# Moving two activation tiles by 896 bytes in on-chip memory, in a two-layer float32 decoder trunk

## Chip, cores and metric

The kernel runs on one core of one Trainium2 chip. The metric is the device time of one execution in microseconds. The inputs are float32, and most products run as three float32r matmuls on split operands (below).

## What is computed

512 tokens of 1,024 channels pass two layers. Layer 0 mixes tokens by a diagonal state-space model with a gated output, layer 1 by differential attention over shared keys and values. Behind each mixer stand a gated feed-forward part and a gated per-layer input. Cut to what matters here:

```python
x = x + s5_mixer(rms_norm(x, ssm_norm))        # w_in, state space, w_glu (1024 x 2048)
k, v = shared_kv(x, kv_norm, kv_w, k_norm)     # layer 1: kv_w (1024 x 2048)
x = x + diff_attention(rms_norm(x, attn_norm), k, v, ...)   # w_q, w_o (1024 x 1024)
for each layer, behind its mixer:
    up = rms_norm(x, ffn_norm) @ w_up          # 1024 x 5632, then a causal convolution of width 3
    x = x + (gelu(g) * val) @ w_down           # 2816 x 1024
    x = x + sigmoid(rms_norm(x, ple_norm) @ w_gate) * (p @ w_proj)
```

## The kernel before

**Products in three parts.** Every large product splits both operands into a float32r part and the float32r rest, and `mm3` (L115 to L120) adds three matmuls into one PSUM bank: high by high (L118), high of the stationary operand by rest of the moving one (L119), and rest by high (L120). Each of them loads a stationary operand of 128x128 and streams a moving operand of 512 columns (256 in a few places).

**Weights.** `stage` (L86) loads a block of 128x1024 into one of five `wst` tiles; `split` (L96) makes the high part on ScalarE (L102 or L107, tile `hi_wst`) and the rest on VectorE (L103 or L108, tile `lo_wst`), six buffers each.

**Activations.** `split_hT` (L160 to L166) writes the transposed activations of all 512 tokens into two constant tiles, `hTh` (high, by ScalarE) and `hTl` (rest, by VectorE), each of 8 k-tiles by 512 tokens, 16 KB a partition. All products with the 1,024 channels read them:
- `up` (the projection up): the weight is stationary, 128 columns of it, and a k-tile of `hTh` or `hTl` moves, 512 tokens.
- `pg` (per-layer gate), `u`, `gv`, `gg` (state-space input, value and gate blocks), `k`, `q`, `v`, `wo` (attention): 128 tokens of `hTh` or `hTl` are stationary, and 512 columns of a weight move. A block of 512 output columns is 4 token tiles x 8 k-tiles x 3 = 96 matmuls.

Two products do without them. `dn` (the projection down) has as stationary operand 128 tokens of `ih` or `il`, tiles of the feed-forward pool, and moves 512 columns of a weight. `pr` (the per-layer input) takes both operands from weight buffers, six matmuls a tile.

**Where tiles lie.** A pool lays its tiles one after another in the order in which they are made, so an address is the sum of what was made before. Start addresses in bytes of a partition, in the built program:

| tile | start | remainder by 256 |
|---|---|---|
| `ident`, `flip`, `junk`, `mhalf` | 16,512 to 19,584 | 128 |
| `x` (16,384 bytes) | 19,648 | 192 |
| `hTh` (16,384) | 36,032 | 192 |
| `hTl` (16,384) | 52,416 | 192 |
| `cw`, `neglam`, `qgain`, `gains` (704 + 32 + 32 + 128) | 68,800 to 69,568 | |
| `wst`, five of 4,096 | from 69,696 | 64 |
| `hi_wst`, six of 4,096 | from 90,176 | 64 |
| `lo_wst`, six of 4,096 | from 114,752 | 64 |
| `ih`, `il`, 14 each of 2,048 | from 164,416 and 193,088 | 64 |

An operand within a tile begins a multiple of 512 bytes behind the tile's start (1,024 where half the tokens move), so the remainder of the tile is that of every operand in it.

**Order of the work.** State space (`ssm`), feed-forward (`ffn`), per-layer input (`ple`), attention, feed-forward, per-layer input. The constant tiles are made in `Trunk.__init__` (L56 to L77); everything else follows from there.

Of the kernel before, what the change touches and what calls it, by code (L numbers as in the profile page):

```python
# [10 lines left out]
F32 = mybir.dt.float32  # L11
F32R = mybir.dt.float32r
# [6 lines left out]
P = 128  # L19
D = 1024  # L20
T = 512
# [12 lines left out]
# k-tiles of the second half of the state-space inputs, by the batch they follow  # L34
# [4 lines left out]
def two_pi_parts():  # L39
    """2 pi as parts of few bits, so that small multiples of the first ones are exact."""  # L40
    a = math.floor(2 * math.pi * 2 ** 9) / 2 ** 9
    b = math.floor((2 * math.pi - a) * 2 ** 21) / 2 ** 21
    return a, b, 2 * math.pi - a - b
# [9 lines left out]
class Trunk:  # L53
    def __init__(self, ctx, tc, io):
        self.tc, self.nc, self.io = tc, tc.nc, io
        nc = self.nc  # L56
        pool = lambda name, **k: ctx.enter_context(tc.tile_pool(name=name, **k))
        self.cpool = pool("const", bufs=1)
        self.wpool = pool("weights", bufs=6)
        self.npool = pool("norm", bufs=2)  # L60
        self.psum = pool("psum", bufs=1, space=PSUM)
        self.ident = self.cpool.tile([P, P], F32, name="ident")
        make_identity(nc, self.ident)
        self.flip = self.cpool.tile([P, P], F32, name="flip")
        self.junk = self.cpool.tile([P, D], BF16, name="junk")
        self.mhalf = self.cpool.tile([P, 16], F32, name="mhalf")
        nc.vector.memset(self.mhalf, -0.5)
        nc.scalar.activation(self.junk[:, :16], self.mhalf, AF.Sin)  # loads the table of the sine
        self.xall = self.cpool.tile([P, NT, D], F32, name="x")
        self.x = [self.xall[:, t, :] for t in range(NT)]  # L70
        self.hTh = self.cpool.tile([P, KD, T], F32R, name="hTh")
        self.hTl = self.cpool.tile([P, KD, T], F32R, name="hTl")
        self.cw = self.cpool.tile([P, 2 * NF, 4], F32, name="cw")
        self.neglam = self.cpool.tile([P, 1], F32, name="neglam")
        self.qgain = self.cpool.tile([P, 1], F32, name="qgain")
        self.gains = self.cpool.tile([P, 4, KD], F32, name="gains")
        self.nw = self.nb = 0  # L77
        self.later, self.turns, self.last = [], [], None
# [7 lines left out]
    def stage(self, src):  # L86
        """Loads [128, 1024] of a weight."""
        st = self.wpool.tile([P, 1024], F32, tag="wst", name=f"wst{self.nw}", bufs=5)
        self.nw += 1
        self.nc.sync.dma_start(st, src)  # L90
        return st
# [4 lines left out]
    def split(self, st, g=None):  # L96
        """A weight in two float32r parts; g: [128, 2], gains of its halves."""
        nc = self.nc
        hi = self.wpool.tile([P, 1024], F32R, tag="whi", name=f"hi_{st.name}")
        lo = self.wpool.tile([P, 1024], F32R, tag="wlo", name=f"lo_{st.name}")  # L100
        if g is None:
            nc.scalar.copy(hi, st)  # L102
            nc.vector.tensor_tensor(lo, st, hi.bitcast(F32), ALU.subtract)  # L103
            return hi, lo
        for k in range(2):
            c = slice(512 * k, 512 * k + 512)
            nc.scalar.activation(hi[:, c], st[:, c], AF.Copy, scale=g[:, k:k + 1])  # L107
            nc.vector.scalar_tensor_tensor(lo[:, c], st[:, c], g[:, k:k + 1], hi[:, c].bitcast(F32),  # L108
                                           ALU.mult, ALU.subtract)
        return hi, lo  # L110
# [11 lines left out]
    def norm(self, nm):  # L122
        """A function of t: the transpose of rms_norm(x) times the gain, for its 128 tokens, into hT."""
# [14 lines left out]
    def flush_turns(self, n=NT):  # L138
        """Emits the transposes of the first n normalized tiles that wait."""
        todo, self.turns = self.turns[:n], self.turns[n:]  # L140
        for f in todo:
            f()
# [9 lines left out]
    def turn(self, x, t, c, nm, tag="tp"):  # L152
        """The half c of the channels of x (128 tokens), transposed, into hT."""
# [6 lines left out]
    def split_hT(self, ps, k, t):  # L160
        """Four transposed blocks into the k-tiles from k on, for the 128 tokens t."""
# [9 lines left out]
    def ffn(self, i, nxt, order=(0, 1), before=None, after=None):  # L171
        """order: of the halves of the tokens at the start. before, after: what else to do on the way."""
# [80 lines left out]
    def ple(self, i, me, nxt=None):  # L253
        """Without nxt the results go out, the last ones in two parts."""
# [38 lines left out]
    # Four steps are a chunk; two groups (32 channels, 128 states) are a pair, four pairs a batch.  # L293
    # State at chunk ends: X[k] = A^4 X[k-1] + V[k]; with X[k] = Z[k] e^(i k phi) and phi the phase
    # of A^4, Z obeys a real recurrence. Outputs: y[4k+i] = C A^(i+1) X[k-1] + sum_j K[i-j] u[4k+j].
# [20 lines left out]
    def ssm_params(self, sp):  # L316
# [50 lines left out]
        # powers of A, as the coefficients of the outputs  # L367
# [18 lines left out]
        # input coefficients f A^(3-j), f = (A - 1) / lambda  # L386
# [12 lines left out]
        # phase of A^4 in turns, as a short and a small part; its multiples by 16 a and by b  # L399
# [27 lines left out]
    def exp(self, x, tl, itile):  # L427
        """e^x to float32's accuracy: 2^n times a polynomial of the rest."""
# [16 lines left out]
    def ssm_tables(self, sp, b):  # L445
        """cos and sin of k phi for the four pairs of a batch, [128, 4, 128]."""
# [22 lines left out]
    def cprod(self, sp, coef, mat, b, nm, conj):  # L469
        """coef[., q, n] * mat[., q, c] (complex) for a batch, [128, 2, 4, n, 16], or its conjugate."""  # L470
# [18 lines left out]
    def pad(self, dst, src):  # L489
        """Block-diagonal form over the two groups of a pair: dst [128, 8, n, 2, 16]."""  # L490
        for g in range(2):
            self.nc.scalar.activation(dst[:, :, :, g, :], src, AF.Copy, scale=self.maskS[:, g:g + 1])
# [6 lines left out]
    def ssm_prep(self, sp, b, coefs):  # L499
        """The stationary and moving operands of a batch: inputs to states, states and inputs to outputs."""  # L500
# [17 lines left out]
    def ssm_toep(self, sp, b, wp, op):  # L518
        """K[0..3] of a pair in the first 32 rows, then the lower rows shifted copies of them."""
# [19 lines left out]
    def ssm_turn_u(self, sp, b, U):  # L539
        """The inputs of a chunk as columns."""  # L540
# [8 lines left out]
    def ssm_inputs(self, b, uc, ctrl):  # L549
        """What the inputs of a chunk add to the states at its end."""  # L550
# [7 lines left out]
    def ssm_states(self, sp, b, v, tab):  # L558
        """The states before each chunk, as two products of the real part and of minus the imaginary part."""
# [27 lines left out]
    def ssm_out(self, sp, b, op, toep, uc, xs):  # L587
        """gelu of the outputs, [chunk, step, channel]."""
# [13 lines left out]
    def ssm_turn(self, b, g):  # L602
        """The k-tile b of the next product."""
# [10 lines left out]
    def ssm(self, nxt):  # L614
        nc, tc, io = self.nc, self.tc, self.io
        with ExitStack() as ctx:
# [3 lines left out]
            # tokens 4 k + j at [k, j]  # L620
# [30 lines left out]
            # software pipeline over the batches  # L651
# [63 lines left out]
    def tables(self):  # L715
        """rel: DRAM scratch [heads, 640]: column m is the bias at distance 511 - m, -1e30 below zero. neglam: [128, 1], minus lambda. qgain: [128, 1] over (c, d), the gain of the scaled query."""
# [20 lines left out]
    def strip(self, dst):  # L737
        """dst[p, h, r] = bias of head h at distance 511 - p - r; p is the place of a query from the end of 128."""
# [10 lines left out]
    def project(self, src, nm, by_tokens, done, gain=None, nxt=None, split=KD // 2):  # L749
        """h @ (a block of 512 columns), one bank for each 128 tokens; done(t, bank) takes them, then nxt."""  # L750
        n = nxt() if nxt else None
        w = self.weights(src, gain)
        if by_tokens:
            # half of the products for all tokens, so that the weights of the next block find room
# [19 lines left out]
    def flush(self, keep=0):  # L774
        """Emits what earlier steps left for the tensor engine to do a little later, but the last keep of it."""
# [5 lines left out]
    def behind(self):  # L781
        """What follows on VectorE waits for a power: queue it behind the last softmax."""
# [11 lines left out]
    def head_norm(self, ps, nb, t, dst, ap, nm, scale, ident, me):  # L794
        """dst[(c, d), head, t] = transposed ps / rms over d (times scale); ident may turn the order of t around."""
# [25 lines left out]
    def attention(self, me, nxt):  # L821
        """Heads 0..3, then 4..7, from the last 128 queries to the first; the products of the second half of the
        keys, values and queries, then those of the outputs, go between the heads."""
# [83 lines left out]
    def heads(self, hb, c, first, todo, done, lag=3):  # L907
        """The four heads of hb for all queries, with steps of todo between them; first comes before the first
        values, done(qb) may add to todo."""
# [31 lines left out]
    def scores(self, qb, h, r0, c):  # L941
        """The two softmaxes of a head, without their sums, the second weighted and subtracted."""
# [34 lines left out]
    def sub_norm(self, qb, hb, po, r0, c):  # L977
        """The outputs of four heads, normalized, take the place of their values of these 128 tokens."""
# [33 lines left out]
class Raw:  # L1012
    """The transpose of x itself into hT, by 128 tokens. The gain goes to the weights; rs, 1 / rms of x, and
    em, eps over its square, go to the outputs."""
# [17 lines left out]
class Accumulate:  # L1032
    """h @ (a block of 512 columns) for all tokens, one k-tile at a time."""
# [14 lines left out]
def onehot():  # L1048
    """[33, 640]: column m picks the T5 bucket of distance 511 - m, or the mask's row."""
# [85 lines left out]
```

## Time and profile before

| | |
|---|---|
| time, median of 3 runs | 1370.0 us (1369.26 to 1370.83) |
| profiled execution, first to last instruction | 1367.3 us |
| TensorE busy | 1346.4 us (98%) |
| its weight loads, beside the matmuls | 1096.2 us (80%) |
| VectorE, ScalarE, GpSimd busy | 787.1, 623.6, 63.8 us |
| granted TensorE clock, mean | 1.000 |

The span of the profiled execution leaves out what lies before the first and behind the last instruction; the median of the runs is 2.7 us above it. Matmuls are pipelined: a row's duration overlaps with the next row's, so the pace of a stream is read from the starts of its rows, not from their durations. In the rows, L115 and the like are lines of the kernel, buffer numbers are left out of the names, and `out<-in` names what an instruction writes and reads.

### The profile page before, as it was taken

To read this page: it belongs to the slowest core of one execution; us is meant where nothing else is said; L and a number is where in the kernel's file an instruction comes from. 1 tells how busy PE (TensorE), PEld (TensorE's weight loads), DVE (VectorE), ACT (ScalarE), POOL (GpSimd) and SP (SyncE) were. 2 spreads that over 40 slices of the span, in tenths; PEclk is the share of its full clock that TensorE was granted. 3 is DMA by queue.
4 is the path that set the end of the run, shared out by engine and by line. 5 is a ranking of instruction groups with operands and counts; after the bars stand their busy time and mean duration, and the time that the engine had idled before them with its cause. 6 is when DMAs were issued, how large, how long until landed. Compare 5 with 4: busy or idle time off the path is not lost.

```text
span 1367.3 us, 16952 instructions
## 1 busy us (share of the span) xinstructions
PE 1346.4 (98%) x6572; PEld 1096.2 (80%) x6572; DVE 787.1 (58%) x1404; ACT 623.6 (46%) x1049; POOL 63.8 (5%) x93
## 2 busy tenths in 40 slices
PE   7999999999999999999999999999999999999998
PEld 6888888988788888888887777678888888888887
DVE  9999833766533565444544765745756434664343
ACT  7988533544421344333535555644444323443241
POOL 1001000000000000000020121000000000000000
PEclk9999999999999999999999999999999999999999
DMA  6121332333333233323333102122333333323311
GB/s 216 59 70 51 110 94 74 101 107 93 93 93 96 89 93 93 110 77 97 107 123 113 59 15 65 60 67 78 119 93 93 108 93 93 94 95 100 97 55 39
DMA packets 37101, 122.34 MB, mean 89 GB/s; under 512 B 4339, under 2 KB 6387, under 8 KB 37020
## 3 DMA queue, kind: packets, MB, share of 16 engines
q1 hardware_dynamic: 35804, 119.07, 28.1%
q10 hardware_dynamic: 1184, 2.16, 0.5%
q8 instruction: 52, 0.85, 0.3%
q14 instruction: 29, 0.24, 0.1%
q0 software_dynamic: 32, 0.02, 0.0%
HBM read 119.12 MB, written 2.12 MB: 89 GB/s over the span
## 4 chain that ended last, share of the span: by engine, by line
PE 87%; DVE 8%; ACT 2%; issue 1%; DMA 1%; POOL 0%; SPq 0%; ACTq 0%; DVEq 0%
PE up L119 12%; PE up L118 12%; PE up L120 12%; PE dn L120 6%; PE dn L118 6%; PE dn L119 6%; PE pg L120 2%; PE pg L118 2%; PE pg L119 2%; PE s L953 2%; PE o L975 1%; DVE zb L576 1%; PE v L118 1%; PE k L118 1%; PE v L120 1%; PE v L119 1%
## 5 line engine op out<-in xcount | busy, mean ns | idle before, releaser
L103 DVE TENSOR_TENSOR lo_wst<-wst,hi_wst 128x1024 fp32r<-128x1024 f32 x162 | 197.8, 1224 | 275.5 <-ACT hi_wst L102 275.5
L119 PE MATMUL up<-hTl,hi_wst 128*128 128x512 f32 (+1 forms) x768 | 289.1, 376 | 0.3 <-DVE hTl L166 0.3
L118 PE MATMUL up<-hTh,hi_wst 128*128 128x512 f32 (+1 forms) x768 | 288.5, 376 | 0.7 <-ACT hTh L165 0.7
L120 PE MATMUL up<-hTh,lo_wst 128*128 128x512 f32 (+1 forms) x768 | 288.6, 376 | 0.0
L102 ACT CAST hi_wst<-wst 128x1024 fp32r<-128x1024 f32 x162 | 169.5, 1047 | 240.9 <-PE dn L120 143.0
L118 PEld LDWEIGHTS up<-hTh,hi_wst 128*128 128x128 f32 x768 | 144.2, 188 | 30.0 <-ACT hTh L165 1.3
L119 PEld LDWEIGHTS up<-hTl,hi_wst 128*128 128x128 f32 x768 | 144.5, 188 | 29.3 <-DVE hTl L166 0.7
L120 PEld LDWEIGHTS up<-hTh,lo_wst 128*128 128x128 f32 x768 | 144.5, 188 | 28.7
L118 PE MATMUL dn<-hi_wst,ih 128*128 128x512 f32 x352 | 137.6, 391 | 0.0
L119 PE MATMUL dn<-lo_wst,ih 128*128 128x512 f32 x352 | 137.0, 389 | 0.0
L120 PE MATMUL dn<-hi_wst,il 128*128 128x512 f32 x352 | 136.4, 389 | 0.0
L242 DVE SCALAR_TENSOR_TENSOR acc<-up,cw,acc 128x511 f32<-128x511 f32 x88 | 65.7, 747 | 52.8 <-ACT acc L241 52.8
L241 ACT ACTIVATE acc<-up,cw 128x512 f32<-128x512 f32 x88 | 68.3, 776 | 53.1 <-PE up L120 53.1
L249 ACT CAST ih<-acc 128x512 fp32r<-128x512 f32 x44 | 27.3, 620 | 112.6 <-DVE acc L246 112.6
L108 DVE SCALAR_TENSOR_TENSOR lo_wst<-wst,gains,hi_wst 128x512 fp32r<-128x512 f32 x80 | 56.4, 747 | 37.9 <-ACT hi_wst L107 37.8
L118 PEld LDWEIGHTS dn<-hi_wst,ih 128*128 128x128 f32 x352 | 66.1, 188 | 14.4 <-issue 0.9
L120 PEld LDWEIGHTS dn<-hi_wst,il 128*128 128x128 f32 x352 | 66.1, 188 | 13.7
L119 PEld LDWEIGHTS dn<-lo_wst,ih 128*128 128x128 f32 x352 | 66.1, 188 | 13.6
L243 DVE SCALAR_TENSOR_TENSOR acc<-up,cw,acc 128x510 f32<-128x510 f32 x88 | 65.8, 748 | 2.9
L107 ACT ACTIVATE hi_wst<-wst,gains 128x512 fp32r<-128x512 f32 x80 | 53.4, 718 | 28.8 <-PE dn L120 16.9
L245 ACT ACTIVATE acc<-acc 128x512 f32<-128x512 f32 x44 | 27.8, 632 | 64.9 <-DVE acc L243 64.9
L120 PE MATMUL pg<-hi_wst,hTl 128*128 128x512 f32 (+1 forms) x128 | 49.8, 389 | 0.0
(276 smaller groups left out, 2256.9 us busy)
## 6 DMA issues: line engine op xcount, KB each, us to landing
wst<-in_w_up SPq DMA_DIRECT2D x88, 512.0 KB, 3.6
wst<-in_w_down SPq DMA_DIRECT2D x44, 512.0 KB, 3.6
wst<-in_w_glu SPq DMA_DIRECT2D x16, 512.0 KB, 3.7
wst<-in_w_gate SPq DMA_DIRECT2D x16, 512.0 KB, 3.6
wst<-in_kv_w SPq DMA_DIRECT2D x16, 512.0 KB, 4.8
wst<-in_w_in SPq DMA_DIRECT2D x8, 512.0 KB, 7.2
wst<-in_w_q SPq DMA_DIRECT2D x8, 512.0 KB, 4.0
wst<-in_w_o SPq DMA_DIRECT2D x8, 512.0 KB, 4.3
```

Source lines behind the costliest of these rows:

```text
L102: nc.scalar.copy(hi, st)
L103: nc.vector.tensor_tensor(lo, st, hi.bitcast(F32), ALU.subtract)
L107: nc.scalar.activation(hi[:, c], st[:, c], AF.Copy, scale=g[:, k:k + 1])
L108: nc.vector.scalar_tensor_tensor(lo[:, c], st[:, c], g[:, k:k + 1], hi[:, c].bitcast(F32), ALU.mult, ALU.subtract)
L118: nc.tensor.matmul(out, ah, bh, start=start, stop=False)
L119: nc.tensor.matmul(out, ah, bl, start=False, stop=False)
L120: nc.tensor.matmul(out, al, bh, start=False, stop=stop)
L241: nc.scalar.activation(c, ps[s], AF.Identity, bias=self.cw[:, n, 3:4], scale=self.cw[:, n, 2:3])
L242: nc.vector.scalar_tensor_tensor(c[:, 1:], ps[s][:, :T - 1], self.cw[:, n, 1:2], c[:, 1:], ALU.mult, ALU.add)
L243: nc.vector.scalar_tensor_tensor(c[:, 2:], ps[s][:, :T - 2], self.cw[:, n, 0:1], c[:, 2:], ALU.mult, ALU.add)
L245: nc.scalar.activation(acc[0], acc[0], AF.Gelu_apprx_tanh)
L953: nc.tensor.matmul(ps[:, :w], qT[r, h, qb * P:(qb + 1) * P], kT[r, h, :w], start=True, stop=True)
```

## The change

The four small tiles `cw`, `neglam`, `qgain` and `gains`, 896 bytes together, are made ahead of `x`, `hTh` and `hTl` in place of behind them. Comments and docstrings are left out as well. The core of the diff:

```diff
         nc.vector.memset(self.mhalf, -0.5)
...
-        self.xall = self.cpool.tile([P, NT, D], F32, name="x")
-        self.x = [self.xall[:, t, :] for t in range(NT)]
-        self.hTh = self.cpool.tile([P, KD, T], F32R, name="hTh")
-        self.hTl = self.cpool.tile([P, KD, T], F32R, name="hTl")
         self.cw = self.cpool.tile([P, 2 * NF, 4], F32, name="cw")
         self.neglam = self.cpool.tile([P, 1], F32, name="neglam")
         self.qgain = self.cpool.tile([P, 1], F32, name="qgain")
         self.gains = self.cpool.tile([P, 4, KD], F32, name="gains")
+        self.xall = self.cpool.tile([P, NT, D], F32, name="x")
+        self.x = [self.xall[:, t, :] for t in range(NT)]
+
+        self.hTh = self.cpool.tile([P, KD, T], F32R, name="hTh")
+        self.hTl = self.cpool.tile([P, KD, T], F32R, name="hTl")
```

In the built program `x` begins at 20,544, `hTh` at 36,928 and `hTl` at 53,312, which all leave 64 by 256; `cw` begins at 19,648, `neglam` at 20,352, `qgain` at 20,384 and `gains` at 20,416. The weight buffers and all else stay where they were. Each engine has the same instructions in the same order with the same waits.

## Rows read from the trace of the kernel before

**Rows 1.** The page: busy time of all engines, granted clock in 40 slices, chain by engine.

```profile
PE 1346.4 (98%) x6572; PEld 1096.2 (80%) x6572; DVE 787.1 (58%) x1404; ACT 623.6 (46%) x1049; POOL 63.8 (5%) x93
...
PEclk9999999999999999999999999999999999999999
...
PE 87%; DVE 8%; ACT 2%; issue 1%; DMA 1%; POOL 0%; SPq 0%; ACTq 0%; DVEq 0%
```

**Rows 2.** Windows of four stretches: start:end, length, then busy us (instructions) per engine, granted clock, DMA.

```profile
0.00:173.00 173.00, 159.39 (x1024) 136.62 (x1025) 159.54 (x368) 141.05 (x252) 14.49 (x47) 1.00 0.31 103
173.00:745.00 572.00, 571.59 (x2625) 468.17 (x2625) 287.74 (x386) 221.20 (x305) 22.46 (x22) 1.00 0.31 95
745.00:934.00 189.00, 187.18 (x934) 137.53 (x932) 121.31 (x378) 105.57 (x290) 23.12 (x18) 1.00 0.19 64
934.00:1367.00 433.00, 428.26 (x1994) 353.89 (x1992) 218.55 (x274) 155.81 (x205) 3.71 (x6) 1.00 0.29 88
```

**Rows 3.** Groups by line and shape, TensorE: count | busy us, mean ns | idle before.

```profile
L118 PE MATMUL up<-hTh,hi_wst 128*128 128x512 f32 x640 | 252.7, 395 | 0.0
...
L118 PE MATMUL dn<-hi_wst,ih 128*128 128x512 f32 x352 | 137.6, 391 | 0.0
...
L119 PE MATMUL up<-hTl,hi_wst 128*128 128x256 f32 x128 | 36.4, 285 | 0.3 <-DVE hTl L166 0.3
...
L157 PE MATMUL tp_ple<-ident,x 128*128 128x128 f32 x64 | 8.6, 273 | 0.0
...
L811 PE MATMUL kt<-ident,kn 128*128 128x128 f32 x32 | 4.8, 272 | 0.0
```

**Rows 4.** Timeline, TensorE, projection down of layer 0: start us, us, instruction.

```profile
410.36 0.39 PE L118 MATMUL dn<-hi_wst,ih 128*128 128x512 f32 x1
...
412.40 0.39 PE L118 MATMUL dn<-hi_wst,ih 128*128 128x512 f32 x1
```

**Rows 5.** Timeline, TensorE, second value block of the gate (gv).

```profile
196.16 0.39 PE L118 MATMUL gv<-hi_wst,hTh 128*128 128x512 f32 x1
...
198.96 0.39 PE L118 MATMUL gv<-hi_wst,hTh 128*128 128x512 f32 x1
```

**Rows 6.** Timeline, TensorE, projection up of layer 0.

```profile
470.21 0.39 PE L118 MATMUL up<-hTh,hi_wst 128*128 128x512 f32 x1
...
472.31 0.40 PE L118 MATMUL up<-hTh,hi_wst 128*128 128x512 f32 x1
```

**Rows 7.** Timeline, TensorE, gate of the per-layer input (pg).

```profile
617.86 0.39 PE L118 MATMUL pg<-hi_wst,hTh 128*128 128x512 f32 x1
...
618.78 0.40 PE L119 MATMUL pg<-lo_wst,hTh 128*128 128x512 f32 x1
619.02 0.40 PE L120 MATMUL pg<-hi_wst,hTl 128*128 128x512 f32 x1
...
619.95 0.39 PE L118 MATMUL pg<-hi_wst,hTh 128*128 128x512 f32 x1
```

**Rows 8.** Windows of 40 us, all engines: down, up, gate.

```profile
395.00:435.00 40.00, 40.00 (x178) 33.14 (x177) 11.31 (x11) 7.38 (x7) 0.00 (x0) 1.00 0.32 104
470.00:510.00 40.00, 40.00 (x173) 32.20 (x172) 24.92 (x31) 15.54 (x21) 0.00 (x0) 1.00 0.33 101
174.00:214.00 40.00, 40.00 (x173) 32.19 (x172) 14.35 (x16) 11.72 (x13) 0.00 (x0) 1.00 0.31 92
```

**Rows 9.** Timeline, TensorE, where up ends and down begins.

```profile
380.28 0.40 PE L118 MATMUL dn<-hi_wst,ih 128*128 128x512 f32 x1
...
382.37 0.39 PE L118 MATMUL dn<-hi_wst,ih 128*128 128x512 f32 x1
...
383.96 0.39 PE L119 MATMUL dn<-lo_wst,ih 128*128 128x512 f32 x1
```

**Rows 10.** Timeline, TensorE, one tile of the per-layer product (pr) between two of pg.

```profile
629.71 0.39 PE L118 MATMUL pr<-hi_wst,hi_wst 128*128 128x512 f32 x1
...
631.09 0.40 PE L118 MATMUL pg<-hi_wst,hTh 128*128 128x512 f32 x1
```

More of the change, by code (lines that the diff above doesn't have):

```diff
@@ L68, in __init__ @@
         nc.scalar.activation(self.junk[:, :16], self.mhalf, AF.Sin)
+        self.cw = self.cpool.tile([P, 2 * NF, 4], F32, name="cw")
+        self.neglam = self.cpool.tile([P, 1], F32, name="neglam")
+        self.qgain = self.cpool.tile([P, 1], F32, name="qgain")
+        self.gains = self.cpool.tile([P, 4, KD], F32, name="gains")
         self.xall = self.cpool.tile([P, NT, D], F32, name="x")
@@ L72, in __init__ @@
         self.hTl = self.cpool.tile([P, KD, T], F32R, name="hTl")
[L73 to L76, printed above, removed]
         self.nw = self.nb = 0
```

## The prediction

> **What bounds the kernel now.** I first read the page and the windows: TensorE is busy 1346.4 us of a span of 1367.3 us, the chain of waits is 87% TensorE, and the granted clock is full in every slice [rows 1]. So nothing can be won by starting TensorE earlier or at a higher clock; what counts is the pace at which it takes matmuls. One stretch is different: up to 173 us, in the state-space part, VectorE is busy 159.5 us and sets the pace. From 173 us on TensorE has hardly a gap: 571.6 of 572 us, then 187.2 of 189 in the attention, then 428.3 of 433 [rows 2].
>
> Then I read the pace itself, by stream, from the starts of the rows. The durations mislead: 395 ns for a matmul of `up`, 391 for one of `dn` [rows 3], while a new one starts every 0.23 us.
> - `dn`: nine matmuls from 410.36 to 412.40, **226.7 ns** each [rows 4].
> - `gv`: twelve from 196.16 to 198.96, **233.3 ns** [rows 5].
> - `up`: nine from 470.21 to 472.31, 233.3 ns [rows 6].
> - `pg`: nine from 617.86 to 619.95, **232.2 ns**, with single steps up to 0.24 us [rows 7].
>
> It is no accident of these microseconds: 40 us of `dn` hold 178 matmuls, 40 us of `up` 173, 40 us of the gate blocks `gg` and `gv` 173 [rows 8].
>
> `dn` and `gv` are the same instruction in the same order: 128 tokens stationary, 512 columns of a weight moving, four banks in turn, three matmuls each. What differs is where the stationary operand lies: `ih` and `il` leave 64 by 256, as the weights do; `hTh` and `hTl` leave 192. `up` has the roles swapped and the same remainders as `gv`, and the same slow pace. Two readings that need no remainder fare badly. *Traffic of the other engines:* VectorE is busy 11.3 us of 40 in `dn`, 14.4 in the gate blocks and 24.9 in `up`; the gate lies by `dn` in this, and its pace is that of `up` [rows 8]. *Some part of the memory that is slow by itself:* the twelve steps of `gv` run through high parts and rests of the weights, 24 KB apart, and through `hTh` and `hTl`, 16 KB apart; a mean of 233.3 ns leaves no room for one kind among them to be fast.
>
> There is a second observation. `dn` does not run at 226.7 ns at once: its first nine matmuls behind `up` take 2.09 us (232 ns each), the next seven 1.59 us (227 ns) [rows 9]. The two operand streams seem to need some matmuls to fall into step. `pr`, with both operands at 64 but only six matmuls long between two `pg`, takes 1.38 us, 230 ns each [rows 10]: on its way to the fast pace, not there.
>
> **The change part by part.** No instruction is added, removed or moved past another; no queue, wait or DMA changes. All that can change is the duration of what reads or writes the moved tiles.
>
> *Matmuls of 512 columns that read `hTh` or `hTl`.* They come to the remainder pair of `dn`, so I price them at 226.7 ns in place of 232.2 to 233.3, a gain of 5.5 to 6.6 ns, **6.1 ns** in the middle (from 232.8). How many:
> - `up` 3 x 640 = 1920 [rows 3]. By the code `pg` has 2 layers x 2 blocks x 96 less the 24 of the one tile that is split, 360; `gg` 192; the second `gv` 96; the first blocks of `k`, `q` and `v` 288. Together 2856, all where TensorE has no gap: 2856 x 6.1 = **17.4 us**.
> - In the attention between the heads: second blocks of `k`, `q`, `v` and both of `wo`, 480, at most 2.9 us. TensorE is busy 187.2 of 189 us there, but scores and values wait in turn for the softmax, so I take two thirds: **1.9 us**.
> - In the state-space part: `u` 192 and the first `gv` 96, at most 1.8 us. VectorE covers it [rows 2]: **0**.
> - Loss while falling into step: about ten matmuls at 232 ns behind each break, 0.055 us; I estimate 20 breaks (starts of stages, transposes between): **-1.1 us**.
>
> *Matmuls of 256 columns* (`up`, 128 in each of three lines, two features at the start of each layer): only rows at the old remainder exist [rows 3]. If they gained the same 2.6% of about 0.12 us, 384 of them give 1.2 us; if nothing, 0. I take 0, since no row shows a fast one.
>
> *Transposes that read `x`.* `tp_ple` reads `x` at 192 and takes 273 ns, `kt` reads `kn` at 64 and takes 272 [rows 3]: 0.
>
> *Writes* of `hTh`, `hTl`, `x` by ScalarE and VectorE: VectorE is busy half the time behind 173 us [rows 2]; a few ns on a copy are covered by matmuls. That cover is gone in the state-space part; its 32 copies into `hTh` and `hTl`, at the 6 ns that the place costs a matmul, would be 0.2 us either way. 0.
>
> *What is late next.* At 2.6% more pace, one feature of `up` (96 matmuls) lasts 21.8 us in place of 22.4. VectorE is busy half the time, the DMA engines 0.32 of it [rows 2, 8]: no new wait.
>
> Sum: 17.4 + 1.9 - 1.1 = 18.2 us. The span goes from 1367.3 to 1349.1, the median of the runs, 2.7 us above it, from 1370.0 to **1351.8 us**.
>
> **A page against the rows.** The rows show that two streams of the same instruction differ by 2.9% in pace with the place of one operand [rows 4, 5]. The Trainium skill's page "SBUF — State Buffer", section "Who interferes with whom", gives TensorE two independent read ports, one for the moving operand and one for weight loads, and says that TensorE never waits on anyone. By that rule the operands' relative place could not matter, the sum would be 0 and the time 1370. The two streams speak against it by 6.6 ns a matmul, so I keep the sum; what the rule would do here is the first rival.
>
> **The rivals.**
> 1. *Nothing happens.* The two streams do not meet, and `dn` is fast for another reason that I don't see, something of its tiles beside the remainder. For it: no row has an `hT` operand at 64. Against: `gv` beside `dn`, the same instruction, and `pr`, which between two `pg` already gains 2 ns a matmul [rows 7, 10]. Then 0 of the 18.2 us come: 1370, within the bound of 0.2% (2.7 us), about what a measurement of this kernel tells from no change.
> 2. *Never in step.* The remainder counts, but `up` changes bank and meets new weights, and falls out of step again and again. Then the stream runs as `dn` does at its start or `pr` does: 230 to 232 ns [rows 9, 10], a gain of 1 to 3 ns on 2856 matmuls, 3 to 8 us: **1362 to 1367**, 1365 in the middle.
> 3. *Slower.* With equal remainders, the weight load and the moving read of `up` begin at the same remainder, with the roles the other way round than in `dn`; such a pair, with the weight part stationary and the activations moving, stands in no row, and the two reads could get in each other's way. If that put every step of `up` at the longest step of `pg`, 240 ns [rows 7], it would cost (240 - 232.8) x 1920 = 13.8 us, less 936 x 6.1 = 5.7 us that the other streams still gain, 8 us in all: **1378**. It decides from the point where `up` has more than 236 ns a step; there its loss (3 ns x 1920) eats that gain. Against it: `up` and `gv` have the same pace now with the roles swapped [rows 5, 6], so the roles seem not to matter.
>
> **How the numbers follow.** In step, as `dn`: 0.68, 1351.8; by itself 1347 (the attention, the state-space part and the 256 columns in full, 22.2 us, and a little for rounding) to 1357 (5.5 ns on the 2856, nothing in the attention, three times the breaks: 15.7 - 3.3 = 12.4 us). Never in step: 0.14. Nothing: 0.11. Slower: 0.07. The first two hold 0.82, so the range goes from 1347 to the end of the second, rounded to **1368**. Faster by over 0.2%: 0.68 + 0.14 = 0.82. Within 0.2%: 0.11. Slower: 0.07.
>
> **What would show it.** In the profile after: starts of `up`, `gv`, `gg` and `pg` 226.7 ns apart, and 177 or 178 matmuls in 40 us of `up` where now there are 173; `dn` as now, but with its first nine matmuls already at 227 ns; the state-space part still 173 us long; the granted clock still full. The forecast is wrong if `up` keeps two paces or 173 matmuls in 40 us, or if `up` falls in step and a new wait for weight parts takes the time back.

## The result, and the profile after

The changed kernel takes 1350.72 us, the median of four runs (1350.32 to 1352.17), beside 1369.92 us for the kernel before in the same measurement. The ratio is 0.9864, with a 95% interval of 0.9852 to 0.9876: **faster by 19.2 us**, where 18.2 had been forecast. The profiled execution spans 1348.5 us (1367.3 before).

Three lines of the page, to be read beside [rows 1]: busy times, granted clock, chain by engine.

```profile
PE 1327.4 (98%) x6572; PEld 1094.7 (81%) x6572; DVE 786.5 (58%) x1404; ACT 623.5 (46%) x1049; POOL 62.9 (5%) x93
...
PEclk9999999999999999999999999999999999999999
...
PE 86%; DVE 10%; ACT 2%; issue 1%; DMA 1%; POOL 0%; SPq 0%; ACTq 0%; DVEq 0%
```

TensorE has lost 19.0 us of busy time (1346.4 to 1327.4); its weight loads, VectorE, ScalarE and the clock are as before. So the time was not won by removing a wait: the same matmuls run in less time, and TensorE is still 98% busy.

The windows of 40 us that answer to [rows 8], in the same order (down, up, gate), with the same columns:

```profile
395.00:435.00 40.00, 40.00 (x178) 33.15 (x177) 11.31 (x11) 7.38 (x7) 0.00 (x0) 1.00 0.33 100
470.00:510.00 40.00, 40.00 (x178) 33.15 (x177) 24.82 (x29) 17.41 (x22) 0.00 (x0) 1.00 0.33 95
174.00:214.00 40.00, 40.00 (x178) 33.15 (x177) 15.16 (x16) 11.07 (x13) 0.00 (x0) 1.00 0.30 92
```

All three now hold 178 matmuls. Before, `dn` alone had 178, and `up` and the gate 173. VectorE is busy 11.3, 24.8 and 15.2 us in them, so the pace does not follow its load.

The steps (a step is the time from the start of one matmul to the start of the next), from the rows in the timeline of the changed kernel, first `gv`, beside [rows 5]. `mm3` stands one line lower there, so its three matmuls are L119 to L121 in place of L118 to L120:

```profile
196.20 0.39 PE L119 MATMUL gv<-hi_wst,hTh 128*128 128x512 f32 x1
...
198.92 0.39 PE L119 MATMUL gv<-hi_wst,hTh 128*128 128x512 f32 x1
```

Twelve matmuls in 2.72 us, 226.7 ns each (233.3 before). Then `up`, beside [rows 6]:

```profile
470.21 0.39 PE L119 MATMUL up<-hTh,hi_wst 128*128 128x512 f32 x1
...
472.25 0.39 PE L119 MATMUL up<-hTh,hi_wst 128*128 128x512 f32 x1
```

Nine in 2.04 us, 226.7 ns (233.3 before). The single steps show more than the mean: of the 1,914 steps of `up` in the trace that join two matmuls of 512 columns without a break (245 ns at most), 1,900 now take 226 or 227 ns; before, not one did, and nearly all lay between 228 and 241. Then the end of `up` and the start of `dn`, beside [rows 9]:

```profile
375.56 0.39 PE L119 MATMUL dn<-hi_wst,ih 128*128 128x512 f32 x1
...
377.60 0.39 PE L119 MATMUL dn<-hi_wst,ih 128*128 128x512 f32 x1
...
379.19 0.39 PE L120 MATMUL dn<-lo_wst,ih 128*128 128x512 f32 x1
```

`dn` now has its fast pace from its first matmul: nine in 2.04 us (2.09 before), the next seven in 1.59 us. And `pr` between two `pg`, beside [rows 10]:

```profile
628.33 0.39 PE L119 MATMUL pr<-hi_wst,hi_wst 128*128 128x512 f32 x1
...
629.46 0.39 PE L121 MATMUL pr<-hi_wst,lo_wst 128*128 128x512 f32 x1
```

Five steps in 1.13 us, 226.6 ns each. The 1.38 us before [rows 10] are six steps, the last of them into `pg`; singly they took 228, 233, 231, 226, 227 and 232 ns. So the first five had a mean of 229 ns, and the fast pace was there from the fourth on.

Where the time came from, by stage, from the starts of the first matmuls of each stage in the two traces:

| stage | before, us | after, us | won | forecast |
|---|---|---|---|---|
| state space, to the first `gg` | 173.1 | 172.4 | 0.7 | 0 |
| gate blocks and the turn to `up` (256 columns) | 94.3 | 92.9 | 1.4 | 1.8 |
| feed-forward 0 | 347.4 | 341.5 | 5.9 | 5.9 |
| per-layer input 0 | 59.3 | 58.1 | 1.2 | 1.2 |
| first `k`, `q`, `v` blocks | 71.5 | 70.1 | 1.4 | 1.8 |
| attention, to the last `wo` | 188.3 | 186.8 | 1.5 | 1.9 |
| turn to feed-forward 1 (256 columns) | 26.0 | 26.2 | -0.2 | 0 |
| feed-forward 1 | 346.0 | 340.2 | 5.8 | 5.9 |
| per-layer input 1 | 61.4 | 60.3 | 1.1 | 1.0 |
| breaks, not placed by the forecast | | | | -1.1 |
| sum | 1367.3 | 1348.5 | 18.8 | 18.2 (of rounded parts 18.4) |

### The profile page after: what moved, and what is told of

It is laid out like the page before. It is cut to its first block, busy times and chain, and to the rows that moved or that the text cites. A ratio compares the mean times of both kernels' runs of the same rounds, so it can differ in the third digit from the quotient of the medians.

```text
span 1348.5 us, 16952 instructions
## 1 busy us (share of the span) xinstructions
PE 1327.4 (98%) x6572; PEld 1094.7 (81%) x6572; DVE 786.5 (58%) x1404; ACT 623.5 (46%) x1049; POOL 62.9 (5%) x93
## 4 chain that ended last, share of the span: by engine, by line
PE 86%; DVE 10%; ACT 2%; issue 1%; DMA 1%; POOL 0%; SPq 0%; ACTq 0%; DVEq 0%
PE up L120 12%; PE up L119 12%; PE up L121 12%; PE dn L119 6%; PE dn L121 6%; PE dn L120 6%; PE pg L121 2%; PE pg L120 2%; PE pg L119 2%; PE s L954 2%; PE o L976 1%; DVE zb L577 1%; PE k L119 1%; PE q L119 1%; PE q L121 1%; PE q L120 1%
## 5 line engine op out<-in xcount | busy, mean ns | idle before, releaser
L104 DVE TENSOR_TENSOR lo_wst<-wst,hi_wst 128x1024 fp32r<-128x1024 f32 x162 | 197.9, 1224 | 268.3 <-ACT hi_wst L103 267.7
L120 PE MATMUL up<-hTl,hi_wst 128*128 128x512 f32 (+1 forms) x768 | 285.6, 372 | 0.3 <-DVE hTl L167 0.3
L119 PE MATMUL up<-hTh,hi_wst 128*128 128x512 f32 (+1 forms) x768 | 285.1, 372 | 0.7 <-ACT hTh L166 0.7
L121 PE MATMUL up<-hTh,lo_wst 128*128 128x512 f32 (+1 forms) x768 | 285.1, 371 | 0.0
L119 PEld LDWEIGHTS up<-hTh,hi_wst 128*128 128x128 f32 x768 | 144.4, 188 | 26.6 <-ACT hTh L166 1.4
L120 PEld LDWEIGHTS up<-hTl,hi_wst 128*128 128x128 f32 x768 | 144.7, 188 | 25.5 <-DVE hTl L167 0.7
L121 PEld LDWEIGHTS up<-hTh,lo_wst 128*128 128x128 f32 x768 | 144.7, 188 | 24.8
L119 PE MATMUL dn<-hi_wst,ih 128*128 128x512 f32 x352 | 137.6, 391 | 0.0
L120 PE MATMUL dn<-lo_wst,ih 128*128 128x512 f32 x352 | 137.0, 389 | 0.0
L121 PE MATMUL dn<-hi_wst,il 128*128 128x512 f32 x352 | 136.4, 389 | 0.0
L119 PEld LDWEIGHTS dn<-hi_wst,ih 128*128 128x128 f32 x352 | 66.1, 188 | 14.5 <-issue 1.0
L121 PEld LDWEIGHTS dn<-hi_wst,il 128*128 128x128 f32 x352 | 66.1, 188 | 13.6
L120 PEld LDWEIGHTS dn<-lo_wst,ih 128*128 128x128 f32 x352 | 66.1, 188 | 13.5
L121 PE MATMUL pg<-hi_wst,hTl 128*128 128x512 f32 (+1 forms) x128 | 49.2, 384 | 0.0
```

The source lines that it names most:

```text
L119: nc.tensor.matmul(out, ah, bh, start=start, stop=False)
L120: nc.tensor.matmul(out, ah, bl, start=False, stop=False)
L121: nc.tensor.matmul(out, al, bh, start=False, stop=stop)
```

## The experiments

The gain was shown; its reason was not. The prediction argued from streams that differ in more than one way: `dn` reads other tiles than `gv`. The theory: **a stream is fast when its stationary and its moving operand leave the same remainder by 256**. Rivals: a tile is good or bad by its own place; the remainder by 512 (or more) counts; `x`, which moved along, has a part; `dn` is fast for a reason of its own. Ten kernels were timed against the kernel before; they differ from it only in where tiles lie, two of them also in a spare tile that VectorE clears once a layer. Each ratio is to the kernel before in the same measurement (medians from 1369.25 to 1369.83 us in the three measurements). The steps are means, in ns, between the starts of the rows of 512 columns in the trace of each run, steps over 245 ns (waits and breaks) left out; `up`, `dn` and `pg` are those of layer 0, `gv` the second block. The second column gives the start of the moving operand less that of the stationary one, by 256.

| run | moving less stationary, by 256: `up` / `gv`, `pg` | `up` | `gv` | `pg` | `dn` | time, us |
|---|---|---|---|---|---|---|
| before | 128 / 128 | 232.8 | 233.3 | 232.9 | 227.0 | 1369.9 |
| changed | 0 / 0 | 226.7 | 226.7 | 227.1 | 226.8 | 1350.7 |
| all at 192 | 0 / 0 | 226.7 | 226.7 | 227.0 | 226.8 | 1351.1 |
| `gains` alone | 0 / 0 (256 by 512) | 226.7 | 226.7 | 226.9 | 226.8 | 1350.8 |
| `ih`, `il` off by 128 | 0 / 0 | 226.7 | 226.7 | 227.0 | **232.8** | 1356.2 |
| 64 | +64 / -64 | 228.9 | 233.3 | 233.3 | 227.0 | 1362.6 |
| 192 | -64 / +64 | 233.3 | 233.3 | 229.0 | 227.1 | 1365.2 |
| 16, minus | -16 / +16 | 234.5 | 228.3 | 227.0 | 226.9 | 1365.5 |
| 16, plus | +16 / -16 | 231.7 | 233.3 | 228.3 | 227.0 | 1363.8 |
| 32 | +32 / -32 | 233.3 | 233.3 | 233.1 | 227.0 | 1370.0 |
| 160 | +160 / +96 | 234.3 | 233.3 | 233.6 | 226.9 | 1373.0 |
| low part alone at 64 | mixed | 228.9 | 233.3 | 233.8 | 227.0 | 1362.3 |

### All operands at 192: is it the place, or the distance?

```diff
-        self.gains = self.cpool.tile([P, 4, KD], F32, name="gains")
+        self.gains = self.npool.tile([P, 4, KD], F32, name="gains", bufs=1)
...
             fp = ctx.enter_context(tc.tile_pool(name=f"ffn{i}", bufs=2))
+            pad = fp.tile([P, 32], F32, name=f"pad{i}", bufs=1)
+            nc.vector.memset(pad, 0.0)
             inter = {}
```

> The activation tiles hTh and hTl stay at remainder 192, as in the kernel before; the weight parts and the feed-forward tiles ih and il are moved to 192 instead (gains is made in a pool behind the weights, a spare tile of 128 bytes stands ahead of the feed-forward tiles). If what counts is that both operands leave the same remainder by 256: all streams of 512 columns 226.7 ns a step, 1351 us. If what counts is the place of a tile by itself (64 good, 192 bad): up, gv and pg at 233 ns as before, and dn slow now too, 1370 + 1056 x 6.1 ns = 1376 us. If the remainder by 512 had to be the same: up, gv, pg and dn all at 233 ns (448 against 192), 1376 us.

Measured: 1351.07 us, ratio to the kernel before 0.9861 (0.9845 to 0.9878). Windows of 40 us on TensorE in the trace of this run: down, up, gate (start:end, length, busy with count, granted clock, DMA).

```profile
390.00:430.00 40.00, 40.00 (x178) 1.00 0.29 93
470.00:510.00 40.00, 40.00 (x178) 1.00 0.27 83
176.00:216.00 40.00, 40.00 (x178) 1.00 0.29 92
```

All three streams run at 178 matmuls in 40 us with `hTh` and `hTl` exactly where they were in the slow kernel. So no tile lay in a bad place; what counts is how the two operands lie to each other. The weight parts are at 448 by 512 here and the activations at 192, so the remainder by 512 need not agree.

### `gains` alone ahead of the activations

```diff
         self.x = [self.xall[:, t, :] for t in range(NT)]
+        self.gains = self.cpool.tile([P, 4, KD], F32, name="gains")
         self.hTh = self.cpool.tile([P, KD, T], F32R, name="hTh")
         self.hTl = self.cpool.tile([P, KD, T], F32R, name="hTl")
...
         self.qgain = self.cpool.tile([P, 1], F32, name="qgain")
-        self.gains = self.cpool.tile([P, 4, KD], F32, name="gains")
```

> The kernel before with gains alone (128 bytes) made ahead of hTh: x stays where it was, hTh and hTl come to remainder 64 by 256 but 320 by 512, the weight parts at 64 by both. If the remainder by 256 decides: 226.7 ns a step in up, gv and pg, 1351 us, and the place of x has no part in the gain. If the remainder by 512 decides: 233 ns, 1370 us. If part of the gain came from x: between the two.

Measured: 1350.83 us, 0.9863 (0.9848 to 0.9878). Up and gate, the same view:

```profile
470.00:510.00 40.00, 40.00 (x178) 1.00 0.31 93
176.00:216.00 40.00, 40.00 (x178) 1.00 0.34 103
```

The whole gain comes with `x` unmoved and with 128 bytes in place of 896. The operands are 256 apart by 512 here and 0 apart in the changed kernel, and both are fast: the remainder by 256 decides, not that by 512.

### Making the fast stream slow

```diff
             fp = ctx.enter_context(tc.tile_pool(name=f"ffn{i}", bufs=2))
+            pad = fp.tile([P, 32], F32, name=f"pad{i}", bufs=1)
+            nc.vector.memset(pad, 0.0)
             inter = {}
```

> The changed kernel with a spare tile of 128 bytes ahead of the feed-forward tiles, so that ih and il leave 192 and the weight parts 64. If equal remainders decide: dn, so far always fast, falls to 232 to 233 ns a step, up stays at 226.7, 1351 + 1056 x 6.1 ns = 1357 us. If dn is fast for another reason: 226.7 ns and 1351 us.

Measured: 1356.20 us, 0.9901 (0.9886 to 0.9915), 5.5 us over the changed kernel. Down, up, gate:

```profile
390.00:430.00 40.00, 40.00 (x174) 1.00 0.31 96
470.00:510.00 40.00, 40.00 (x178) 1.00 0.28 87
176.00:216.00 40.00, 40.00 (x178) 1.00 0.34 104
```

The roles are turned round: `dn`, 178 or 179 in every other run, falls to 174, and `up` and the gate keep 178. Nothing about `dn` was fast by itself. 1056 matmuls x 5.8 ns (mean of both layers, 232.6 less 226.8 ns) make 6.1 us; the 5.5 measured show nearly all of it on the path.

### Half-way distances: 64 and 192

```diff
+        self.cw = self.cpool.tile([P, 2 * NF, 4], F32, name="cw")
         self.hTh = self.cpool.tile([P, KD, T], F32R, name="hTh")
...
-        self.cw = self.cpool.tile([P, 2 * NF, 4], F32, name="cw")
```

> The kernel before with cw alone made ahead of hTh: hTh and hTl at remainder 128, 64 off the weight parts. If every distance that is no multiple of 256 costs the same: about 233 ns a step and 1370 us. If the cost grows with the distance: between 227 and 233 ns, 1351 to 1370 us. If only a distance of 128 hurts: 226.7 ns, 1351 us.

Measured: 1362.56 us, 0.9946 (0.9931 to 0.9961): about 40% of the gain, and not evenly. `up`, 24 matmuls in the timeline:

```profile
475.21 0.39 PE L118 MATMUL up<-hTh,hi_wst 128*128 128x512 f32 x1
...
480.70 0.39 PE L118 MATMUL up<-hTh,hi_wst 128*128 128x512 f32 x1
```

5.49 us, 228.8 ns a step. `gv`, 24 matmuls:

```profile
203.28 0.39 PE L120 MATMUL gv<-hi_wst,hTl 128*128 128x512 f32 x1
...
208.88 0.39 PE L120 MATMUL gv<-hi_wst,hTl 128*128 128x512 f32 x1
```

5.60 us, 233.3 ns. The two streams have the same two remainders with the roles exchanged, so either the role counts or the sign of the distance, if the distance alone decides. The next run exchanges them.

```diff
+        self.neglam = self.cpool.tile([P, 1], F32, name="neglam")
+        self.qgain = self.cpool.tile([P, 1], F32, name="qgain")
         self.hTh = self.cpool.tile([P, KD, T], F32R, name="hTh")
...
-        self.neglam = self.cpool.tile([P, 1], F32, name="neglam")
-        self.qgain = self.cpool.tile([P, 1], F32, name="qgain")
```

> The kernel before with neglam and qgain ahead of hTh: hTh and hTl at remainder 0, the weight parts at 64. The moving operand lies 64 short of the stationary one in up and 64 past it in gv, gg, pg: the run with hTh at 128 with the roles exchanged. If the signed distance from the stationary to the moving operand decides: up at 233.3 ns (as gv there), gv and gg at 228.9 (as up there), 1350.7 + 1920 x 6.6 + 1416 x 2.2 ns = 1367 us. If the role decides and not the sign (up bears a distance better than gv): up at 228.9, gv at 233.3, 1362.6 us as there.

Measured: 1365.21 us, 0.9968 (0.9955 to 0.9981). First `up`, 24 matmuls, then `gv`, 24, then `pg`, 18 up to the first of `pr`:

```profile
475.22 0.39 PE L120 MATMUL up<-hTh,lo_wst 128*128 128x512 f32 x1
...
480.82 0.39 PE L120 MATMUL up<-hTh,lo_wst 128*128 128x512 f32 x1
```

```profile
203.25 0.40 PE L119 MATMUL gv<-lo_wst,hTh 128*128 128x512 f32 x1
...
208.85 0.40 PE L119 MATMUL gv<-lo_wst,hTh 128*128 128x512 f32 x1
```

```profile
631.99 0.39 PE L118 MATMUL pg<-hi_wst,hTh 128*128 128x512 f32 x1
...
636.11 0.39 PE L118 MATMUL pr<-hi_wst,hi_wst 128*128 128x512 f32 x1
```

`up` takes 233.3 ns and `pg` 228.9 (4.12 us by 18): that is the sign. But `gv`, which has the same pair of remainders as `pg`, stays at 233.3. Neither expectation holds as a whole.

### 16 bytes, both ways

The two parts become one tile, begun 16 bytes into it; in the first run that leaves `up` at -16, in the second `gains` and `neglam` go ahead as well and it has +16.

```diff
-        self.hTh = self.cpool.tile([P, KD, T], F32R, name="hTh")
-        self.hTl = self.cpool.tile([P, KD, T], F32R, name="hTl")
+        both = self.cpool.tile([P, 2 * KD * T + 8], F32R, name="hT")
+        self.hTh, self.hTl = (both[:, 4 + n * KD * T:4 + (n + 1) * KD * T].rearrange("p (k t) -> p k t", k=KD) for n in range(2))
```

> The changed kernel with hTh and hTl as two parts of one tile, begun 16 bytes into it: remainder 80, all behind them 32 bytes on, at 96. The moving operand lies 16 short of the stationary one in up, 16 past it in gv, gg, pg. If the sign counts down to small distances: up at 233 ns, gv at 227, 1350.7 + 1920 x 6.6 ns = 1363 us. If 16 bytes are too few to matter: 226.7 ns in all, 1351 us.

Measured: 1365.53 us, 0.9972 (0.9962 to 0.9981). Up and gate:

```profile
470.00:510.00 40.00, 40.00 (x173) 1.00 0.35 105
176.00:216.00 40.00, 40.00 (x177) 1.00 0.29 92
```

173 in `up`, 177 in the gate: 16 bytes off are enough to lose the pace in `up`, and most of it is kept in the other role. The sign again, it seems, with 2.5 us more lost than forecast.

> The kernel before with gains and neglam ahead of one tile that holds both parts, begun 16 bytes into it: hTh and hTl at remainder 112, the weight parts, ih and il at 96. The moving operand lies 16 past the stationary one in up and 16 short of it in gv, gg, pg: the run with 16 bytes with the roles exchanged. If the signed distance decides: up at 228.3 ns, gv and gg at 233 to 234, 1350.7 + 1920 x 1.7 + 1416 x 6.6 ns = 1363 us. If the role decides: up at 233.3 to 234.5, gv at 228.3, 1365.5 us as there.

Measured: 1363.76 us, 0.9956 (0.9942 to 0.9970). In this run `pg` and `v` are the same instruction with the same pair of remainders. `pg`, 18 matmuls, then `v`, 18:

```profile
631.97 0.39 PE L120 MATMUL pg<-hi_wst,hT 128*128 128x512 f32 x1
...
636.05 0.39 PE L120 MATMUL pg<-hi_wst,hT 128*128 128x512 f32 x1
```

```profile
732.17 0.40 PE L118 MATMUL v<-hi_wst,hT 128*128 128x512 f32 x1
...
736.37 0.40 PE L118 MATMUL v<-hi_wst,hT 128*128 128x512 f32 x1
```

4.08 us against 4.20: 226.7 ns and 233.3 ns a step, at the same distance, in the same execution. These are stretches: all 190 steps of `pg` have a mean of 228.3 ns. So with unequal remainders a stream has more than one pace that it can hold, and the distance alone does not say which. What came before the stream may, but no run here varies that by itself. `up`, expected at 228.3, had 231.7, and `pg`, counted in the sum at 6.6 ns over the fast pace, had 1.6. So the median near the 1363 us of the first expectation does not bear it out. The traced execution was the longest of the five (1365.96 us; the shortest took 1363.28), so the paces in the others may differ.

### 32 and 160

Both move small tiles only, as above: `gains` and `neglam` ahead of `hTh` in the first, `neglam` alone in the second.

> The kernel before with gains and neglam ahead of hTh: hTh and hTl at remainder 96, the weight parts at 64. The moving operand lies 32 past the stationary one in up and 32 short of it in gv, gg, pg. If the sign counts, as the run with 64 suggests (up 228.9, gv 233.3 ns) and the cost rises with how far the moving one lies past: up at 227 to 228 ns, gv at 233, 1350.7 + 1920 x 1.1 + 1416 x 6.6 ns = 1362 us at most. If only the size of the distance counts: all at 227 to 228 ns, 1352 to 1354 us. A step under 226.7 ns anywhere would mean that equal remainders are not the best place.

Measured: 1370.04 us, 1.0007 (0.9998 to 1.0016). Up and gate:

```profile
470.00:510.00 40.00, 40.00 (x173) 1.00 0.34 105
176.00:216.00 40.00, 40.00 (x173) 1.00 0.30 92
```

A miss: 32 past costs `up` as much as 128 does, though 64 past costs a third of it. The cost does not grow with the distance. No stream of 512 columns has a mean step under 226.7 ns in any run, so nothing here speaks for a place better than equal for them.

> The kernel before with neglam alone ahead of hTh: hTh and hTl at remainder 224, the weight parts at 64. The moving operand lies 160 past the stationary one in up, 96 past in gv, gg, pg (256 less 160). If the cost rises with how far it lies past, 2.3 ns at 64 and 6.2 at 128: gv between them, 229 to 232 ns, up at 233, 1367 to 1370 us. If only the size counts, 96 either way: up and gv alike.

Measured: 1373.04 us, 1.0031 (1.0019 to 1.0042).

```profile
470.00:510.00 40.00, 40.00 (x172) 1.00 0.34 105
176.00:216.00 40.00, 40.00 (x174) 1.00 0.31 93
```

`gv` was not in between but at 233.3, and `up`, at 234.3 ns, was slower than in the kernel before: 3 us over the end of what was expected, and 3.8 us over the kernel before in the same measurement (1369.25 us). With 32 bytes in another place the kernel is slower than before, with 128 it is 19 us faster; between the worst and the best order of the same tiles lie 22 us.

### The low part alone

```diff
         self.hTh = self.cpool.tile([P, KD, T], F32R, name="hTh")
+        self.gains = self.cpool.tile([P, 4, KD], F32, name="gains")
         self.hTl = self.cpool.tile([P, KD, T], F32R, name="hTl")
...
-        self.gains = self.cpool.tile([P, 4, KD], F32, name="gains")
```

> The kernel before with gains between hTh and hTl: hTh stays at 192, hTl comes to 64, as the weight parts. If each step pays for its own pair of operands (moving one, and the load that runs beside it): one step of three has an equal pair, about a third of the gain, 1364 us. If a stream has to fall into step as a whole, and a mixed one cannot: no gain, 1370 us.

Measured: 1362.25 us, 0.9952 (0.9935 to 0.9969). Up and gate:

```profile
470.00:510.00 40.00, 40.00 (x177) 1.00 0.29 90
176.00:216.00 40.00, 40.00 (x173) 1.00 0.31 93
```

Neither expectation: the gate gets nothing (173), `up` two thirds of its gain (177, 228.9 ns). The means hide single steps. From the starts in the trace, sorted by the line that begins the step, `up` takes 232.5 (L118), 225.8 (L119) and 228.4 ns (L120), and the gate block `gg` 233, 232 and 235. In both, L119 begins the step in which the moving operand and the weight load beside it (that of the next matmul) both leave 64. So `up` does not move as a whole: its equal step is the fast one, but one of the others gains too; in the gate the equal step is the shortest by 1 ns and the sum gains nothing.

No kernel beat the changed one by more than the runs scatter; the first two are as fast.

## Why the prediction was right

**The bound.** That TensorE's pace sets the time from 173 us on was right: the busy time fell by 19.0 us and the span by 18.8.

**The comparison of `dn` and `gv`.** The forecast rested on one difference between two streams of the same instruction, the remainder by 256. It was an argument from one pair; the runs make it a finding. Moving the weights to the activations does what moving the activations to the weights does, 128 bytes do what 896 do, and `dn` can be made slow by the same 128 bytes.

**The sum.** The gain per matmul was taken as 6.1 ns; in `up` it is 232.8 - 226.7 = 6.1, in `gv` 6.6. Up: 11.7 us forecast, 11.7 measured in the two feed-forward parts. Gate and first `k`, `q`, `v` blocks: 1.8 each, measured 1.4 each. In `k`, `q` and `v` the breaks that the forecast had put in one term of -1.1 are seen: the steps of their first blocks have means of 227.5 to 228.2 ns and not 226.7, which is 0.36 us. Attention: 1.9, measured 1.5. The term that failed, by little, is that of the state-space part: priced at 0 behind VectorE, it gave 0.7 us; without it the sum is 18.1 us where 18.2 had been forecast. VectorE is as busy there as before (159.5 us), but it does not cover the first `u` block: between 17 and 37 us of the trace before, TensorE and VectorE are both busy 20.00 of 20.00 us, and from its first to its last matmul the block takes 26.3 us in place of 27.0. One bound was also rounded the wrong way: 1370.0 less 12.4 is 1357.6, not 1357.

**What was priced at nothing.** Matmuls of 256 columns gained nothing. Their durations are 285 ns before [rows 3] and 286 after; their steps, which count, even rose from 118.7 to 119.8 ns, 0.4 us over the 369 steps without a break. With `up` at -64 they have 115.8 ns, so for them equal remainders are not the best of the places tried. The transposes of `x` did not change: 273 ns on both sides, and the run with `x` in its old place is as fast. No new wait came up: TensorE is idle 21.1 us of the span (1348.5 less 1327.4) and was idle 20.9 before, and VectorE waits for ScalarE's high parts 267.7 us in place of 275.5.

**Falling into step.** What was forecast came: `dn` starts fast now. That it does so because `up` ahead of it has the same pace is not shown, and one run speaks against it. With the parts at -16, `up` has 234.5 ns and `dn` starts at 226.7 all the same:

```profile
382.10 0.40 PE L120 MATMUL up<-hT,lo_wst 128*128 128x512 f32 x1
382.33 0.39 PE L118 MATMUL dn<-hi_wst,ih 128*128 128x512 f32 x1
...
384.37 0.39 PE L118 MATMUL dn<-hi_wst,ih 128*128 128x512 f32 x1
```

And slow steps come back behind a break with no change of pace: in the changed kernel the 18th step of `dn` is 308 ns long, and the next six take 231, 231, 236, 228, 233 and 230 ns before 227 is back. Nor is the number fixed: in the trace before, the second stretch of `dn` (from 557.71 us) has three slow steps, not nine.

**The rivals.** *Nothing happens* falls: the same instruction takes a step of 226.7 or 233.3 ns by where its two operands lie to each other, with the other engines' work unchanged. The Trainium skill's page "SBUF — State Buffer", section "Who interferes with whom", has the two read ports of TensorE independent and TensorE waiting on nobody; what the prediction worked out from it, that the place could not matter, does not hold in this case, and the measurement decides. *Never in step* did not come: 1,900 of 1,914 steps of `up` are in step. *Slower* was wrong in its mechanism: `up` at equal remainders is as fast as `dn`. A pace slower than before does exist at another distance: `up` at 160 has 234.3 ns, far from the 240 of the rival, and that kernel is slower than before by 0.31%.

**What stays open.** Why 256, and what the two reads do to each other. At other distances a stream holds one of several paces, between 226.7 and 234.5 ns; neither the size nor the sign of the distance orders them, and the same distance gave two paces in one execution. That the weight load and the moving read get in each other's way is the likely reading, since only the distance of their operands was varied; no view shows the reads themselves. That each step pays for its own pair was expected of the run with the low part alone, and held for one step of `up` and not for the gate.

## What to carry to other kernels

Where TensorE is full, read the distance between the starts of matmuls in each stream, not their durations, and compare streams of the same instruction; a difference of 3% that follows the tiles, not the neighbours, points to where the operands lie. Lay the stationary and the moving operands of float32r matmuls of 512 columns so that they leave the same remainder by 256 bytes (those of 256 columns did not gain); here that is a matter of the order in which small tiles are made, and it costs nothing. Look at it again after any change in the size of a tile that lies ahead of them: 32 bytes more were enough to lose all of it (`gains` alone ahead: 1350.8 us; `gains` and `neglam`: 1370.0).

## What the runs showed of the hardware that was not expected

- The pace of a stream of float32r matmuls of 512 columns depends on the distance of its two operands in a partition. At a granted clock of 1.00 (2.4 GHz) a step takes 226.7 ns, 544 cycles, at multiples of 256 bytes, and mostly 233.3 ns, 560 cycles, elsewhere.
- 16 bytes off are enough (`up` at -16: 234.5 ns in layer 0, 233.3 in layer 1), and the cost does not grow with the distance: +64 cost `up` 2.2 ns, +32 cost 6.6, both from 226.7.
- With equal remainders the steps are even, 226 or 227 ns for hundreds of matmuls; with a distance of 128 they are not, 228 to 241 ns in `up`. Behind a break or another stream `dn` needs none to ten steps to reach its pace, and the pace of the stream ahead does not say how many.
- At one and the same distance, -16, 18 matmuls of `pg` held 226.7 ns and 18 of `v` 233.3 in one execution.
